# Dummy products, smaller first loads, second-scale sums between blocks, and a last row tile on VectorE in a hybrid encoder layer

## The chip, the cores and the metric

The kernel runs on one core of a Trainium2 chip. The metric is device time in microseconds (us), the median of repeated runs. A core has five engines that run their own instruction streams and wait for each other through semaphores: TensorE (PE in the profile; its weight loads are listed apart as PEld), VectorE (DVE), ScalarE (ACT), GpSimd (POOL) and SyncE (SP), which here only issues transfers. Sixteen DMA engines carry the transfers.

## The reference

One layer of an encoder, batch 1, 1024 positions, width 2048, float32 throughout:

```
h   = rmsnorm(x, pre_g) * (1 + scale(c)) + shift(c)      # shift, scale, gate = silu(c) @ w_ada + b_ada
q, k, v, gate_a, u, gate_p = split(h @ w_in)              # w_in: 2048 x 4608
y_a = windowed_attention(q, k, v; relative bias, sink) * silu(gate_a)
y_p = multi_scale_pool(u) * silu(gate_p)
g   = sigmoid(h @ w_merge + b_merge)                      # 2048 x 4096
m   = g_a * (y_a @ w_br_attn) + g_p * (y_p @ w_br_pool)
out = x + gate(c) * rmsnorm(m @ w_out, post_g)
```

## The kernel before

Every large product keeps float32 accuracy by splitting both operands into a high part and a low rest (`hi`, `lo`) and adding three products, high by high, low by high and high by low. ScalarE makes the high part (a copy to `F32R`), VectorE the low one (source minus high). Most products are also done by a seven-product scheme on 2 x 2 blocks (`strassen`); TensorE runs these nearly without a gap from about 80 us to the end.

The change concerns the two ends of the program.

**The ramp.** Before `h` is known, the kernel has to load x (8 MB) and to get the modulation. It avoids waiting for either. `fetch_scales(j)` loads the columns of `w_ada` for the scale of 256 channels (pair j: contraction tiles k = 2j and 2j + 1) as eight tiles of 256 KB. `row_sums` multiplies them with silu(c) on TensorE: step q takes four of the sixteen contraction tiles (two transfers), with four of them side by side in column groups of the array; the last step copies the sums to `acc` on ScalarE, and the step after it (`sum_columns`) transposes them (PM), reduces them on VectorE, and `scale_columns` writes the factors `modc`. Meanwhile x is loaded and transposed on TensorE (`turn_part`, line 502, into `XT`), and `raw_operands` multiplies the transposed tile with its `modc` column while it splits it: the high part on ScalarE (line 695), the low on VectorE (line 696). So the products of the first 256 output columns (key and value columns of `w_in`, the `wide` tiles) can run on scaled, not yet normalized x (`plain_block`, line 833; `PB` in the profile). The factors of the rows follow when all of x has been squared (`square_of`, `norm_row`, `factors`), and are spread over columns by two products with `ones` (`spread_factors`, RB). From then on the modulation for further channels, the transposes of the rest and the first `strassen` products (`ramp_gen`) follow.

A `plain_block(i, blk, j)` makes one 128 x 512 block from six products: number n = 0 and 1 are high by high for the two contraction tiles kh = 0 and 1 of pair j, 2 and 3 use the low weights, 4 and 5 the low x. Block "11" and "21" are for the first 512 positions, "12" and "22" for the last 512. Operand names: B11 and B21 are the two contraction tiles for the first positions, B12 and B22 those for the last.

Instructions wrapped in `keep` stay in the order in which the program writes them, on each engine; this holds for nearly all of the ramp. All loads of the ramp go through SP's queue, in program order. In the head this order is: the eight tiles of scale 0; columns 0 to 255 of x for the first four row tiles (four transfers of 128 KB); the first 256 columns of `wide`; columns 0 to 511 of the last four row tiles (256 KB each); columns 256 to 511 of the first four; the other 256 columns of `wide`; the eight tiles of scale 1; the next `wide` tile; then the remaining columns of x.

**The end.** `out_pair` makes the last output rows. For the last two row tiles (t = 0, 1), once the last product is there, `square` sums its squares on ScalarE, `scale_of` gives the row factor, and each of the four 512-column blocks is finished by `r * scale + x` and stored. `finish_block` does this in one VectorE instruction and stores through SP's queue; for one block of the very last tile `finish_apart` does it with ScalarE (multiply), GpSimd (add) and ScalarE's queue (store).

The lines that the steps below speak of: 539 products of `row_sums`, 543 `acc`, 523 transposes of the sums, 695/696 `raw_operands`, 562 loads of scales, 437 loads of x columns (`fetch_halves`), 847 `put_by`, 187 loads of weights for `strassen`, 96 the high part in `split`, 293 the copy into Z in `strassen`, 1737/1738 `finish_block`, 1742 to 1744 `finish_apart`.

## Time and profile before

| | |
|---|---|
| runs | 2085.36, 2086.59, 2087.91 us; median 2086.59 |
| profiled execution | 2086.87 us; its span 2085.1 us |
| busy: TensorE, VectorE, ScalarE, GpSimd | 2066.5, 1566.2, 1112.1, 39.4 us |
| chain of work that ended last | TensorE 93%, DMA 3%, VectorE 2%, ScalarE 1% |
| granted TensorE clock | 0.999 |
| DMA | 476.61 MB, mean 229 GB/s |

How to read the lines below. A line of the timeline is: start in us from the span's start, length in us, engine, line of the kernel, operation, `out<-in` by the program's names, shapes, count (xN merges N instructions that follow each other), and in brackets how long the engine sat idle before it and what ended that. A q behind an engine (SPq) marks an instruction of its queue, such as the issue of a transfer. A matmul in float32 appears as two instructions. A line of the table by stretch is: the stretch, its length, the busy time of PE, PEld, DVE, ACT and POOL with the number of instructions, the granted clock, the DMA share and GB/s. A line of waits is: who waited, for whom, us in total, times, longest. A line of transfers is: `out<-in`, queue, count, size, median us from issue to landing.

### The profile page before, as it was taken

The numbers are of one execution on the slowest core, as the hardware profiler recorded it, in microseconds if no ns is written. First come the engines' busy times: TensorE is split into PE (matmuls) and PEld (weight loads), VectorE is DVE, ScalarE is ACT, GpSimd is POOL, SyncE is SP. The second block draws the span as 40 slices with busy tenths as digits, with TensorE's granted clock in tenths as the row PEclk, the third lists the DMA queues.
The fourth block names the chain that finished last, engine by engine and source line by source line (L and its number), as shares of the span: only waits on it lengthen the run. The fifth ranks groups of instructions, "written<-read, shape, count | busy, mean of one in ns | idle before, by whom it ended". The sixth has DMA issues, their size and how long they took to land.

```text
span 2085.1 us, 29058 instructions
## 1 busy us (share of the span) xinstructions
PE 2066.5 (99%) x9527; PEld 1701.9 (82%) x9527; DVE 1566.2 (75%) x2822; ACT 1112.1 (53%) x2121; POOL 39.4 (2%) x133
## 2 busy tenths in 40 slices
PE   8999999999999999999999999999999999999998
PEld 6678888888888888888888888888888888888886
DVE  5889688776565876777777788858858977889667
ACT  5764444444664634656665443334645645768554
POOL 0100000000000000000000000010000000000000
PEclk9999999999999999999999999999999999999999
DMA  9978877887575477655554576675654556786996
GB/s 342 357 269 268 267 248 249 291 287 227 189 236 168 161 260 257 205 166 176 183 169 149 179 235 224 201 243 191 227 168 162 189 186 205 239 295 211 299 335 231
DMA packets 303137, 476.61 MB, mean 229 GB/s; under 512 B 24026, under 2 KB 140402, under 8 KB 302984
## 3 DMA queue, kind: packets, MB, share of 16 engines
q1 hardware_dynamic: 297472, 459.63, 67.2%
q0 software_dynamic: 4304, 12.75, 1.6%
q10 hardware_dynamic: 1208, 2.37, 0.3%
q8 instruction: 75, 1.23, 0.2%
q14 instruction: 78, 0.64, 0.1%
HBM read 346.70 MB, written 130.05 MB: 229 GB/s over the span
## 4 chain that ended last, share of the span: by engine, by line
PE 93%; DMA 3%; DVE 2%; ACT 1%; issue 0%; SPq 0%; DVEq 0%; ACTq 0%
PE Z L237 31%; PE V L237 21%; PE X L237 20%; PE Z L1704 2%; PE Z L1706 2%; PE Z L1705 2%; PE X L1704 1%; PE V L1706 1%; PE X L1706 1%; PE V L1704 1%; PE V L1705 1%; PE X L1705 1%; DMA raw<-in_w_merge_dram 1%; PE PB L833 1%; PE PT L1414 1%; DMA raw<-in_w_in_dram 1%
## 5 line engine op out<-in xcount | busy, mean ns | idle before, releaser
L96 ACT ACTIVATE whi<-raw 128x512 fp32r<-128x512 f32 (+1 forms) x528 | 314.6, 600 | 490.4 <-PE Z L237 245.5
L97 DVE TENSOR_TENSOR wlo<-raw,whi 128x512 fp32r<-128x512 f32 (+1 forms) x528 | 339.5, 648 | 135.9 <-PE Z L237 102.5
L97 DVE TENSOR_TENSOR wlo<-wr,whi 128x512 fp32r<-128x512 f32 x224 | 150.5, 688 | 52.1 <-ACT whi L96 49.2
L96 ACT ACTIVATE whi<-wr 128x512 fp32r<-128x512 f32 x224 | 138.4, 629 | 87.6 <-DVE wlo L97 29.6
L103 DVE TENSOR_TENSOR raw<-raw,raw 128x512 f32<-128x512 f32 x76 | 52.4, 690 | 89.7 <-DMA raw<-in_w_merge_dram 59.6
L96 ACT ACTIVATE whi<-ws 128x512 fp32r<-128x512 f32 (+1 forms) x88 | 53.0, 602 | 71.3 <-PE X L237 62.3
L237 PE MATMUL V<-T3h,whi 128*128 128x512 f32 x328 | 89.6, 392 | 1.0 <-DVE u L103 0.9
L237 PE MATMUL Z<-B22h,whi 128*128 128x512 f32 x328 | 89.6, 392 | 0.0
L237 PE MATMUL Z<-T1h,whi 128*128 128x512 f32 x328 | 89.6, 390 | 0.0
L237 PE MATMUL X<-B21h,whi 128*128 128x512 f32 x328 | 89.5, 391 | 0.0
L237 PE MATMUL Z<-T2h,wlo 128*128 128x512 f32 x328 | 88.9, 390 | 0.6 <-DVE wlo L97 0.6
L237 PE MATMUL X<-B11h,whi 128*128 128x512 f32 x328 | 89.4, 390 | 0.0
L237 PE MATMUL Z<-T2h,whi 128*128 128x512 f32 x328 | 89.0, 390 | 0.4 <-ACT Z L293 0.3
L237 PE MATMUL V<-T4h,whi 128*128 128x512 f32 x328 | 89.3, 391 | 0.0
L237 PE MATMUL X<-B11l,whi 128*128 128x512 f32 x328 | 89.2, 390 | 0.0
L237 PE MATMUL Z<-B22l,whi 128*128 128x512 f32 x328 | 88.9, 390 | 0.0
L237 PE MATMUL Z<-T1l,whi 128*128 128x512 f32 x328 | 88.9, 389 | 0.0
L237 PE MATMUL V<-T3l,whi 128*128 128x512 f32 x328 | 88.9, 390 | 0.0
L237 PE MATMUL X<-B21l,whi 128*128 128x512 f32 x328 | 88.9, 390 | 0.0
L237 PE MATMUL V<-T4l,whi 128*128 128x512 f32 x328 | 88.8, 390 | 0.0
L237 PE MATMUL V<-T4h,wlo 128*128 128x512 f32 x328 | 88.8, 390 | 0.0
L237 PE MATMUL X<-B11h,wlo 128*128 128x512 f32 x328 | 88.8, 390 | 0.0
(423 smaller groups left out, 4910.9 us busy)
## 6 DMA issues: line engine op xcount, KB each, us to landing
part<-part_d SPq DMA_DIRECT2D x136, 256.0 KB, 4.9
ada<-in_w_ada_dram SPq DMA_DIRECT2D x128, 256.0 KB, 5.9
raw<-in_w_merge_dram SPq DMA_DIRECT2D x64, 512.0 KB, 5.3
wr<-ws_dS SPq DMA_DIRECT2D x60, 512.0 KB, 5.5
raw<-in_w_in_dram SPq DMA_DIRECT2D x56, 512.0 KB, 4.3
wr<-in_w_out_dram SPq DMA_DIRECT2D x48, 512.0 KB, 5.5
proj_d<-part SPq DMA_DIRECT2D x68, 256.0 KB, 2.3
sw<-in_w_out_dram SPq DMA_DIRECT2D x64, 256.0 KB, 5.3
```

The lines of the kernel that those rows point to most:

```text
L96: ins = (nc.scalar.activation(hi, src, AF.Copy), nc.vector.tensor_tensor(lo, src, f32(hi), ALU.subtract))
L97: nc.vector.tensor_tensor(lo, src, f32(hi), ALU.subtract))
L103: return (eng or nc.vector).tensor_tensor(o, a, b, ALU.add)
L237: nc.tensor.matmul(ps, w_[:, i], op[mov][j][m_], start=fresh and i == 0 and n == 0, stop=i == nj - 1 and n == 2, skip_group_check=True)
L833: keep(nc.tensor.matmul(opened[i, blk], w[:, kh, nt * P:(nt + 1) * P], mov[kh][m], start=j == n == 0, stop=j == 1 and n == 5, skip_group_c ...
L1414: nc.tensor.transpose(pt[:, i * P:(i + 1) * P], p[:, i * P:(i + 1) * P], ident)
L1704: nc.tensor.matmul(pb, hi, w[0], start=first, stop=False, skip_group_check=True)
L1705: nc.tensor.matmul(pb, lo, w[0], start=False, stop=False, skip_group_check=True)
L1706: nc.tensor.matmul(pb, hi, w[1], start=False, stop=last, skip_group_check=True)
```

## The change

- Before the first product, six dummy products of `ones` by `ones` (128 x 128, float32) are put on TensorE, then three more after the transpose of c, and one more after each of the first two steps of the first scale's sums. `ones` is set by VectorE instead of GpSimd for that, ahead of `scz`.
- The first columns of x and of `wide` are loaded by contraction tile: columns 0 to 127 of four row tiles and the weights of the first contraction tile, then columns 128 to 255 and the second. The last four row tiles come in halves of 256 columns. Weights and x operands are split by contraction tile too (`first_weights`, `raw_operands` with `khs`).
- The first scale's sums (`g[4]`) are put ahead of the first transposes of x. The product numbers of the first two blocks run in the order 0, 2, 4, 1, 3 and then 5, where it was 0, 2, 1, 3 and then 4, 5.
- The second scale's sums are put between blocks: two steps, the six products of block "11", two steps, four products of block "21", the transposes of the sums, the last two products. The two `square_of` steps that stood ahead of them come after. The high weights of the second 256 columns (`wide_weights(1, 0)`) are made before the transposes instead of after them.
- `finish_apart` goes; `finish_block` does all four blocks of the last row tile, in the order 0, 2, 3, 1.

```diff
@@ -385,9 +385,9 @@
     fetch_rows(rows, b_ada[0, 0:2 * D], pre_g[0])
     nsink_t = const.tile([P, NH], F32, name="nsink_t")
     scz = xa2.tile([P, KT, 32], F32, name="scz")
+    ones = xa2.tile([P, P], F32, name="ones")
+    nc.vector.memset(ones, 1.0)
     nc.vector.memset(scz, 0.0)
-    ones = xa2.tile([P, P], F32, name="ones")
-    nc.gpsimd.memset(ones, 1.0)
     b1 = xa2.tile([P, 4], F32, name="b1")
     shz = xa2.tile([P, 4, 32], F32, name="shz")
     nc.gpsimd.memset(shz, 0.0)
@@ -430,11 +430,11 @@
             xts[si, q] = slot("xt", F32)
             keep(load(xts[si, q], x[si * P:(si + 1) * P, q * 512:(q + 1) * 512]))
 
-    def fetch_halves(h):
-        for si in range(4):
-            if h == 0:
+    def fetch_cols(sis, c0, c1):
+        for si in sis:
+            if (si, 0) not in xts:
                 xts[si, 0] = slot("xt", F32)
-            keep(load(xts[si, 0][:, h * 256:(h + 1) * 256], x[si * P:(si + 1) * P, h * 256:(h + 1) * 256]))
+            keep(load(xts[si, 0][:, c0:c1], x[si * P:(si + 1) * P, c0:c1]))
 
     def claim_turned(ks):
         for k in ks:
@@ -686,9 +686,10 @@
 
     right = {}
 
-    def raw_operands(j, s, turned=False):
-
-        for kh, name in enumerate(("B11", "B21") if s == 0 else ("B12", "B22")):
+    def raw_operands(j, s, turned=False, khs=(0, 1)):
+
+        for kh in khs:
+            name = (("B11", "B21") if s == 0 else ("B12", "B22"))[kh]
             k = 2 * j + kh
             src, a = tbanks[s, k] if turned else xT[k, s], modc[:, 1, kh, j:j + 1]
             hi, lo = right[j] if name == "B12" else op[name][j]
@@ -764,25 +765,34 @@
 
     raws, wide = [], {}
 
-    def fetch_wide(half, j, n1=0, n2=512):
-
-        if n1 == 0:
+    def fetch_wide(half, j, n1=0, n2=512, k0=0, k1=2):
+
+        if n1 == k0 == 0:
             wide[half, j] = wp.tile([P, 2, 512], F32, tag="raw", name=uid("wide"), bufs=4)
         n0 = COL_K + half * 512
-        keep(load(wide[half, j][:, :, n1:n2],
-                  w_in[2 * j * P:(2 * j + 2) * P, n0 + n1:n0 + n2].rearrange("(k p) n -> p k n", p=P)))
-
+        keep(load(wide[half, j][:, k0:k1, n1:n2],
+                  w_in[(2 * j + k0) * P:(2 * j + k1) * P, n0 + n1:n0 + n2].rearrange("(k p) n -> p k n", p=P)))
+
+    def warm(n):
+
+        b = bank("at", "WARM")
+        for _ in range(n):
+            keep(nc.tensor.matmul(b[:, 0:P], ones, ones, start=True, stop=True))
+
+    warm(6)
     pc = bank(SEEDED[1], "pc")
     keep(nc.tensor.transpose(pc[:, 0:16], crow, ident[0:16, 0:16]))
     keep(nc.scalar.activation(scz[:, :, 0], pc[:, 0:16], AF.Silu))
     keep(nc.scalar.activation(sc, pc[:, 0:16], AF.Silu))
+    warm(3)
     scales = [fetch_scales(0)]
-    fetch_halves(0)
-    fetch_wide(0, 0, 0, 256)
-    for si in range(4, 8):
-        fetch_row(si, (0,))
-    fetch_halves(1)
+    for k in range(2):
+        fetch_cols(range(4), k * P, (k + 1) * P)
+        fetch_wide(0, 0, 0, 256, k, k + 1)
+    fetch_cols(range(4, 8), 0, 256)
     fetch_wide(0, 0, 256, 512)
+    fetch_cols(range(4, 8), 256, 512)
+    fetch_cols(range(4), 256, 512)
     claim_turned(range(4))
     for j in range(2):
         claim(j, ("B11", "B21", "B22"))
@@ -806,14 +816,18 @@
 
     weights0 = {}
 
-    def wide_weights(i, j, by_vector=False):
+    def first_weights(kh):
+        if kh == 0:
+            weights0[0, 0] = [wp.tile([P, 2, 256], F32R, tag=t, name=uid(t), bufs=4) for t in ("whi", "wlo")]
+        hi, lo = (t[:, kh] for t in weights0[0, 0])
+        keep(nc.vector.tensor_copy(hi, wide[0, 0][:, kh, 0:256]))
+        low_weights(lo, wide[0, 0][:, kh, 0:256], hi)
+
+    def wide_weights(i, j):
         hi, lo = (wp.tile([P, 2, 256], F32R, tag=t, name=uid(t), bufs=4) for t in ("whi", "wlo"))
         src = wide[i // 2, j][:, :, i % 2 * 256:i % 2 * 256 + 256]
         weights0[i, j] = hi, lo
-        if by_vector:
-            keep(nc.vector.tensor_copy(hi, src))
-        else:
-            keep(nc.scalar.activation(hi, src, AF.Copy))
+        keep(nc.scalar.activation(hi, src, AF.Copy))
         return partial(low_weights, lo, src, hi)
 
     def low_weights(lo, src, hi):
@@ -847,12 +861,6 @@
         keep(nc.scalar.activation(t, opened.pop((i, blk)), AF.Copy))
         nc.gpsimd.dma_start(block(ramp_d[i], 0)(blk), t)
 
-    def warm(n):
-
-        b = bank("at", "WARM")
-        for _ in range(n):
-            keep(nc.tensor.matmul(b[:, 0:P], ident, ident, start=True, stop=True))
-
     BLOCKS = ("11", "21", "12", "22")
 
     given = []
@@ -881,27 +889,29 @@
         plain_block(i, blk, 1)
 
     g = row_sums(scz, scales[0], partial(scale_columns, 0), 2)
-    g[0]()
-    g[1]()
+    for q in range(2):
+        g[q]()
+        warm(1)
     g[2]()
     small_vectors()
     g[3]()
+    g[4]()
     turn_part(0, (0,), SEEDED[:1])
-    g[4]()
     turn_part(0, (1,), SEEDED[1:])
-    wide_weights(0, 0, True)()
-    raw_operands(0, 0, True)
+    for kh in range(2):
+        first_weights(kh)
+        raw_operands(0, 0, True, (kh,))
     for k in range(2):
         take_turned(0, k, k == 1)
     PAIR = (("11", "sc"), ("21", "sc"))
     for blk, tag in PAIR:
         plain_block(0, blk, 0, tag, (0,))
-    for n in (2, 1, 3):
+    for n in (2, 4, 1, 3):
         for blk, _ in PAIR:
             plain_block(0, blk, 0, None, (n,))
     turn_part(1, (0, 1), ("at", "at"))
     for blk, _ in PAIR:
-        plain_block(0, blk, 0, None, range(4, 6))
+        plain_block(0, blk, 0, None, (5,))
     raw_operands(0, 1, True)
     for k in range(2):
         take_turned(1, k, k == 1)
@@ -910,27 +920,30 @@
         plain_block(0, blk, 0, tag, range(2))
     for blk, _ in PAIR:
         plain_block(0, blk, 0, None, range(2, 6))
+    low = wide_weights(1, 0)
     turn_part(1, (2, 3), ("at", "at"))
     turn_part(0, (2, 3), SEEDED)
     for n in (1, 0):
         for k in (2, 3):
             take_turned(n, k, k == 3)
-    wide_weights(1, 0)()
+    low()
+    g = row_sums(scz, scales[1], partial(scale_columns, 1), 2)
+    g[0]()
+    g[1]()
+    plain_block(1, "11", 0, SEEDED[0])
+    g[2]()
+    g[3]()
+    plain_block(1, "21", 0, SEEDED[1], range(4))
+    g[4]()
+    plain_block(1, "21", 0, None, range(4, 6))
     for si in range(2):
         square_of(si, 0, si % 2 == 1)
-    g = row_sums(scz, scales[1], partial(scale_columns, 1), 2)
-    for step in g[:4]:
-        step()
-    plain_block(1, "11", 0, SEEDED[0], range(2))
-    g[4]()
     wide_weights(0, 1)()
     raw_operands(1, 0)
     raw_operands(1, 1)
     for si in range(2, 8):
         square_of(si, 0, si % 2 == 1)
     keep(nc.scalar.activation(ep.tile([P, 1], F32, name="root"), eps_t, AF.Sqrt))
-    plain_block(1, "11", 0, None, range(2, 6))
-    plain_block(1, "21", 0, SEEDED[1])
     wide_weights(1, 1)()
     norm_row(0)
     plain_block(0, "11", 1)
@@ -1737,12 +1750,6 @@
         keep(nc.vector.scalar_tensor_tensor(r, r, scale, xrow.pop((T, n)), op0=ALU.mult, op1=ALU.add))
         store(rows_of(T, n), r)
 
-    def finish_apart(T, n, scale):
-        r = held.pop((T, n))
-        keep(nc.scalar.activation(r, r, AF.Copy, scale=scale))
-        nc.gpsimd.tensor_tensor(r, r, xrow.pop((T, n)), ALU.add)
-        nc.scalar.dma_start(rows_of(T, n), r)
-
     def fetch_x_block(T, n, tile_of):
         xrow[T, n] = tile_of("xr")
         return load(xrow[T, n], x[T * P:(T + 1) * P, n * 512:(n + 1) * 512])
@@ -1866,9 +1873,7 @@
                 out_mm(bz[t], op, "B22", j, t, w, False, j == len(last_weights) - 1)
             result("12", t, bz[t], c12[t])
             scale = scale_of(6 + t, rest[t])
-            if t == 1:
-                finish_apart(6 + t, 3, scale)
-            for n in (0, 2, 1) if t == 1 else (0, 2, 3, 1):
+            for n in (0, 2, 3, 1):
                 finish_block(6 + t, n, scale)
 
     nextm, nextt2 = [], {}
```

## The prediction

> **What bounds the kernel now.** I read the page's busy table and chain first, then a table by stretch, then the waits of TensorE, then the timelines of the first 80 us and the last 15.
>
> ```profile
> span 2085.1 us, 29058 instructions
> PE 2066.5 (99%) x9527; PEld 1701.9 (82%) x9527; DVE 1566.2 (75%) x2822; ACT 1112.1 (53%) x2121; POOL 39.4 (2%) x133
> PE 93%; DMA 3%; DVE 2%; ACT 1%; issue 0%; SPq 0%; DVEq 0%; ACTq 0%
> ...
> 9.50:14.50 5.00, 4.02 (x28) 1.91 (x24) 1.73 (x7) 1.21 (x3) 0.00 (x0) 1.00 0.94 301
> 16.00:20.00 4.00, 3.92 (x22) 2.94 (x21) 2.55 (x5) 1.96 (x4) 0.00 (x0) 1.00 1.08 360
> 40.00:65.00 25.00, 25.00 (x128) 17.77 (x127) 20.96 (x45) 19.21 (x42) 4.15 (x27) 1.00 1.05 393
> 65.00:98.00 33.00, 32.56 (x174) 23.93 (x173) 26.26 (x60) 24.40 (x50) 4.25 (x8) 1.00 1.08 361
> 98.00:110.00 12.00, 12.00 (x72) 7.69 (x71) 9.63 (x22) 8.59 (x17) 0.00 (x0) 1.00 0.43 150
> ```
>
> TensorE is busy for 99% of the span and is 93% of the chain. The change touches only the first 30 us and the last 10. In the stretches (length, then busy time of each engine, granted clock, DMA share, GB/s) from 16 to 98 us the DMA engines are full (1.05 to 1.08); after that they have room (0.43). So there are two runners in the first 98 us, TensorE and the DMA, and a head start of one alone is worth nothing if the other decides a wait later. The profiled execution took 2086.87 us, 1.77 more than its span, and 0.28 more than the median of the runs, 2086.59.
>
> ```profile
> PE Z L237 <- ACT Z L293: 0.3, 1, 0.3
> ...
> 64.42 0.60 ACT L847 ACTIVATE c<-PB 128x512 f32<-128x512 f32 x1 [1.20 <-PE PB L833]
> 65.54 0.42 ACT L96 ACTIVATE whi<-raw 128x256 fp32r<-128x256 f32 x1 [0.51 <-DMA raw<-in_w_in_dram]
> ...
> 77.26 0.74 PE L237 MATMUL Z<-T2h,whi 128*128 128x512 f32 x2 [0.29 <-ACT Z L293]
> ```
>
> One of the few waits that the profile counts for TensorE in the first 90 us is 0.3 us at 77.26, for ScalarE's copy into Z. The chain leads from that copy back to 65.54, where ScalarE sat 0.51 us idle until a `raw` transfer landed; before it ScalarE had copied `c` at 64.42, for which it had waited 1.20 us on TensorE. So at 65.54 the DMA decides, and TensorE's own work is only 0.51 us behind it. What the head of the kernel is worth is settled there.
>
> **The change, part by part.**
>
> *Dummy products (six, three, one and one, 128 columns each).*
>
> ```profile
> 3.77 1.85 PE L539 MATMUL GEMV<-ada,scz 128*32 128x256 f32 x8 [0.29 <-ACT sc L778]
> 6.95 3.73 PE L539 MATMUL GEMV<-ada,scz 128*32 128x256 f32 x16 [1.32 <-DMA ada<-in_w_ada_dram]
> 10.85 0.84 PE L539 MATMUL GEMV<-ada,scz 128*32 128x256 f32 x8
> ...
> ada<-in_w_ada_dram SPq DMA_DIRECT2D x1, 256.0 KB, 6.7
> ...
> 50.51 1.88 PE L490 MATMUL RB<-diag,ones 128*128 128x512 f32 x4
> ```
>
> Two tiles of the first scale take 1.85 us at the start and 0.84 us at 10.85: products run at half rate until about 10.8 us, although the granted clock reads 1.00 throughout. No row shows a dummy; the nearest are the float32 sums at 50.51, two products of 512 columns in 1.88 us, so 128 columns take 0.24 us, or 0.47 at half rate. Nine before the first tile are 2.1 to 4.2 us from about 1.1 us on (when `ones` is set), so they end by 5.3 at the latest; two tiles at 0.93 more is 7.2, against 6.95, where the third tile's products start after 1.32 us of waiting for the DMA. The eighth tile's transfer is issued at about 4.3 us and lands 6.7 us later, at 11.0; the last group runs there already at full rate. So the dummies can win nothing at its end: the cover is the landing of the scale tiles. I take 0; bounds 0 and +0.2 (should the last dummy delay the eighth tile's products). If that landing came sooner, they would be worth at most the 0.5 us by which one tile is slower at half rate (0.93 against 0.42).
>
> *Sums before the transposes; x and weights by contraction tile.*
>
> ```profile
> 11.73 0.38 ACT L543 ACTIVATE acc<-GEMV 128x256 f32<-128x256 f32 x1 [7.95 <-PE GEMV L539]
> 12.66 0.38 PE L523 MATMUL PM<-ident,acc 128*128 128x128 f32 x2
> 14.41 0.73 PE L833 MATMUL PB<-B11h,whi 128*128 128x512 f32 x2 [0.93 <-ACT B11h L695]
> 16.35 1.03 PE L502 MATMUL XT<-ident,xt 128*128 128x128 f32 x8
> 17.37 0.69 ACT L695 ACTIVATE B12h<-XT,modc 128x512 fp32r<-128x512 f32 x1 [1.28 <-PE XT L502]
> ```
>
> The sums (PM) could start when `acc` is done, at 12.1, but stand behind four transposes that wait for x; now they go first: 12.66 becomes 12.16, and modc, B11h and the first product come 0.5 us earlier, 13.9. Then the gain goes: two low products now precede the eight transposes at 16.35, and B12h waits for those. Before, 14.41 to 16.35 held eight products (1.94 us); now ten (2.4): 13.9 + 2.4 = 16.3. B12h (0.69 us of ScalarE) stays at 17.3 and the next blocks, which wait for it, at 18.1. Gain at 18.1: 0.05, taken as 0. VectorE casts half a tile twice instead of one whole; its sum is the same.
>
> The price is on SP's queue. Between the first scale tiles and the second there were 14 transfers; now there are 23, of the same bytes: eight of 64 KB instead of four of 128, and more halves.
>
> ```profile
> SPq L437 <- DMA ada<-in_w_ada_dram: 1.4, 2, 0.8
> ...
> 11.88 0.90 SPq L437 DMA_DIRECT2D xt<-in_x_dram  x2
> 14.45 4.91 SPq L562 DMA_DIRECT2D ada<-in_w_ada_dram  x8
> 2079.73 0.33 SPq L1738 DMA_DIRECT2D out_dram<-c  x1
> ...
> ada<-in_w_ada_dram SPq DMA_DIRECT2D x1, 256.0 KB, 5.0
> out_dram<-c SPq DMA_DIRECT2D x1, 256.0 KB, 2.5
> ```
>
> The issues of x wait for landings of scale tiles (1.4 us, two waits); the issue times fit a limit of eight transfers under way, so smaller ones put fewer bytes under way. By the landing of the eighth tile (11.0) both kernels have issued eight more. Before, six others followed and the second scale started at 14.45. Now fifteen follow, at a pitch of 0.47 us (two in 0.90 at 11.88): 11.4 + 15 x 0.47 = 18.45. A tile of the second scale landed 5.0 us after its issue because some 2 MB stood ahead of it; with less ahead it can land after 2.5, as the last store does: 20.95 against 19.45. So everything behind on this full queue is 1.5 us late, up to the `raw` transfer at 65.54. Bounds: 0 (a pitch of 0.37, from the 0.33 of the last store's issue: 11.4 + 5.55 + 2.5 = 19.45) and +2.0 (0.50). I take +1.5, since the issues at 11.88 are of the same rows. DMA path at 65.54: +1.5.
>
> By the Trainium skill, page "DMA: Bandwidth & Descriptors", section "Measured (HBM→SBUF, 128 partitions, SWDGE, issued from GpSimd)", a 64 KB transfer reaches 138 GB/s; as an estimate from that figure, eight of them one at a time are 3.8 us where the full rate needs 1.5, and the DMA path would be +3.8 in place of +1.5. No row here shows a 64 KB transfer.
>
> *Second scale's sums between blocks.*
>
> ```profile
> 23.16 2.11 PE L539 MATMUL GEMV<-ada,scz 128*32 128x256 f32 x32
> 25.78 0.42 PE L523 MATMUL PM<-ident,acc 128*128 128x128 f32 x2
> 26.83 0.72 ACT L695 ACTIVATE B11h<-xT,modc 128x512 fp32r<-128x512 f32 x1 [0.23 <-DVE modc L550]
> 28.34 0.39 PE L833 MATMUL PB<-B11h,whi 128*128 128x512 f32 x1
> ...
> 36.13 0.58 ACT L837 ACTIVATE held<-PB 128x512 f32<-128x512 f32 x1
> 36.76 0.50 PE L833 MATMUL PB<-B12h,whi 128*128 128x512 f32 x1
> ```
>
> Before: 32 products to 25.2, two of block "11", the sums at 25.78, then ten products of cover, and B11h of the second pair at 26.83; TensorE uses it at 28.34. Now six products stand between the halves and four behind them, so the sums start after ten block products, not two: 23.16 + 2.0 + 10 x 0.23 = 27.4, and B11h at 28.45, with only two products of cover. That is +1.6 for B11h, which TensorE now waits for. From there ScalarE works nearly without a gap to the copy at 36.13 that TensorE waits for at 36.76, so +1.6 passes on. It saves about 0.3 us of waits for the last scale tiles, inside that number, and it covers the tiles' later landing: the eighth is needed 1.4 us later than before. At 64.42 the ScalarE copy comes +1.6 late: it ends at 66.6, 1.1 past 65.54. TensorE path there: +1.1; bounds 0 (should idle time between 36.8 and 64 take it up) and +1.6.
>
> At 65.54 the later one counts: max(+1.5, +1.1) = +1.5. From there to 77.26 and on nothing in the change makes it up.
>
> *Last row tile by VectorE alone.*
>
> ```profile
> 2073.24 0.75 DVE L1737 SCALAR_TENSOR_TENSOR c<-c,st,xr 128x512 f32<-128x512 f32 x1
> ...
> 2076.62 1.41 DVE L1737 SCALAR_TENSOR_TENSOR mo<-mo,st,xr 128x512 f32<-128x512 f32 x2
> 2077.43 1.73 POOL L1743 TENSOR_TENSOR p<-p,xr 128x512 f32<-128x512 f32 x1 [56.82 <-ACT p L1742]
> 2077.95 1.75 DVE L1737 SCALAR_TENSOR_TENSOR c<-c,st,xr 128x512 f32<-128x512 f32 x1
> ```
>
> The last VectorE step took 1.75 us beside GpSimd's addition, where the same step took 0.75 at 2073.24. Now four steps follow from 2076.62: 1.41 for two and 0.67 for each of two more, 2.75 in all, so 2079.37 instead of 2079.70: -0.33. Bounds: 0 (should the last step stay at 1.75 by its own doing) and -1.0 (the whole difference of 1.75 to 0.75). The last store no longer meets one of ScalarE's queue: another -0.1, an estimate. I take -0.4.
>
> **Sum.** +1.5 - 0.4 = +1.1: 2086.87 becomes 2088.0 in the profile, and the median 2087.7.
>
> **The rivals.**
> 1. *The head is hidden.* Issues take 0.37 and idle time takes up ScalarE's lateness (VectorE and ScalarE are busy 0.84 and 0.77 of 40 to 65 us); then only the tail is left: -0.4, 2086.2. Against it: 0.5 us at 65.54 is all the slack that the rows show.
> 2. *The head gains.* The DMA wins back what it lost from 9.5 to 14.5 (301 GB/s against 360 after), the `raw` transfer lands sooner, and the 0.51 us at 65.54 goes: -0.9, 2085.7. More it can't be, since ScalarE's copy of `c` ends there at 65.0.
> 3. *Slower by over 0.2%.* The small transfers run at latency, eight at a time: if each takes the 5.0 us of the row above, eight in 5.0 are 0.62 each; fifteen are 9.4 us, the second scale is issued at 20.8 and, if it again lands 5.0 later, is 6.3 late: 2086.6 + 6.3 - 0.4 = 2092.5. It decides from 4.6 us of lateness on. For it: the queue did wait for landings. Against it: those 5.0 us are mostly bytes ahead, since the last store takes 2.5. With the Trainium skill's figure above for 64 KB the time would lie between, 2090.0.
>
> **How the numbers follow.** Forecast 0.58, head hidden 0.2, head gains 0.1, latency 0.07, elsewhere 0.05. The likeliest gives 2087.7 (its own range 2086.7 to 2088.7). Head gains at 2085.7 less the 0.4 by which a median of such runs wanders gives the low end, 2085.3; 2.0 of DMA lateness with 0.5 of other waits and the same 0.4 gives 2089.6. A measurement tells 0.2%, 4.2 us; so the first three cases are the same by it, the latency is slower, and of elsewhere 0.02 is faster and 0.01 slower: faster 0.02, same 0.90, slower 0.08.
>
> **What would show it.** The first product near 13.9 and B12h still at 17.3; 23 issues between the scales, the second scale's first issue near 18.4 and its landing near 21; B11h of the second pair near 28.4 with a TensorE wait of about 0.8 us before it; the `raw` copy of 65.54 near 67; Z of 77.26 near 78.8; the last step of 0.75 us. It is wrong if the first issue of the second scale stays below 16.5, if Z is at 77.3 or earlier, or if TensorE's time between 98 us and the last product changes by more than 0.5 us.

## The result, and the profile after

The median of the changed kernel is 2090.88 us (2088.29 to 2093.76, ten runs) against 2085.97 for the kernel before on the same chip; ratio 1.0021, 95% interval 1.0012 to 1.0029, so 2.5 to 6.0 us slower. The forecast was 2087.7. Run again later, unchanged, it gave 2089.23 against 2087.53, ratio 1.0013 (1.0003 to 1.0024). The profiled execution took 2091.53 us. From its page:

```profile
span 2089.7 us, 29111 instructions
PE 2072.7 (99%) x9549; PEld 1705.7 (82%) x9549; DVE 1567.1 (75%) x2826; ACT 1111.4 (53%) x2120; POOL 37.5 (2%) x131
```

Its table by stretch (length, busy time of PE, PEld, DVE, ACT, POOL with counts, granted clock, DMA share, GB/s):

```profile
9.50:14.50 5.00, 4.14 (x25) 2.51 (x25) 2.92 (x10) 2.24 (x4) 0.00 (x0) 1.00 0.70 197
16.00:20.00 4.00, 3.62 (x17) 2.33 (x16) 2.00 (x3) 2.38 (x4) 0.00 (x0) 1.00 0.90 275
40.00:65.00 25.00, 25.00 (x123) 17.60 (x122) 20.07 (x47) 20.47 (x47) 4.07 (x27) 1.00 1.05 393
65.00:98.00 33.00, 32.75 (x180) 24.25 (x177) 26.16 (x59) 24.32 (x49) 4.35 (x11) 1.00 1.09 363
98.00:110.00 12.00, 12.00 (x70) 7.68 (x69) 10.79 (x23) 9.48 (x20) 0.00 (x0) 1.00 0.64 226
```

TensorE is again busy for 99%. The loss stands in the first two stretches: the DMA engines, at 301 and 360 GB/s before, move 197 and 275, with a share of 0.70 and 0.90. From 40 us on they are as full as before, so what was lost is not won back; more is left over for 98 to 110 (0.64 in place of 0.43).

The timeline of SP's queue (start, time spent issuing, number), and further down of what waits for those transfers:

```profile
11.49 1.85 SPq L437 DMA_DIRECT2D xt<-in_x_dram  x4
13.38 0.43 SPq L773 DMA_DIRECT2D wide<-in_w_in_dram  x1
13.86 3.79 SPq L437 DMA_DIRECT2D xt<-in_x_dram  x8
17.69 4.91 SPq L562 DMA_DIRECT2D ada<-in_w_ada_dram  x8
...
13.11 0.73 PE L847 MATMUL PB<-B11h,whi 128*128 128x512 f32 x2 [0.20 <-DVE wlo L106]
16.82 0.69 ACT L696 ACTIVATE B12h<-XT,modc 128x512 fp32r<-128x512 f32 x1 [2.26 <-PE XT L502]
27.42 1.31 PE L539 MATMUL GEMV<-ada,scz 128*32 128x256 f32 x8 [0.37 <-DMA ada<-in_w_ada_dram]
30.70 0.72 ACT L696 ACTIVATE B11h<-xT,modc 128x512 fp32r<-128x512 f32 x1 [0.41 <-DVE modc L550]
31.47 0.49 PE L847 MATMUL PB<-B11h,whi 128*128 128x512 f32 x1 [0.94 <-ACT B11h L696]
68.28 0.60 ACT L861 ACTIVATE c<-PB 128x512 f32<-128x512 f32 x1 [1.20 <-PE PB L847]
68.86 0.42 ACT L96 ACTIVATE whi<-raw 128x256 fp32r<-128x256 f32 x1
80.67 0.73 PE L237 MATMUL Z<-T2h,whi 128*128 128x512 f32 x2 [0.25 <-ACT Z L293]
```

The transfers of the first 30 us (number, size, median us from issue to landing):

```profile
xt<-in_x_dram SPq DMA_DIRECT2D x12, 128.0 KB, 3.4
xt<-in_x_dram SPq DMA_DIRECT2D x8, 64.0 KB, 2.8
```

Once the first scale has landed (10.15), SP waits for no landing before 17.69 (the view of its waits from 10.5 to 17.7 us is empty) and issues these loads at one pitch, whatever their size: (13.38 - 11.49) / 4 = 0.47 us and (17.69 - 13.86) / 8 = 0.48 for 128 KB, 0.48 for the 256 KB at 13.38, 0.475 for the last of 64 KB (10.54 to 11.01 in the trace). 128 KB at this pitch are some 275 GB/s offered, 64 KB 138, while the engines could move 350 (e3 below, 10 to 14 us). They stand idle for want of requests. Small pieces are not slow on the engines themselves: those that SP had issued while the scale tiles were still under way landed one behind the other, from 10.73 to 11.61 three of 64 KB and one of 128 KB, which is 372 GB/s (landings from the trace). The second scale, first issued at 17.69 (14.45 before), has its last tile at 28.06 (24.61 before, from the trace's landings). TensorE waits for its last two tiles at 27.42, then 0.94 us for B11h at 31.47, and Z of 77.26 comes at 80.67.

On the way to Z both runners of the prediction are late. ScalarE's copy of `c` starts 37.6 us behind the second B11h in all 14 profiles of this document, so TensorE's path passes on all of its lateness: 64.42 became 68.28, +3.9, where 0.5 was slack. The `raw` transfer landed at 65.51 before and at 68.84 here, +3.3. The copy of `raw`, 65.54 before, comes at 68.86, when both are there.

The dummies did bring TensorE to full rate sooner. In the kernel before, every product of the first scale up to 10.1 us took 0.63 us, and those from 10.85 on 0.38 to 0.40; here they take 0.38 to 0.40 from 7.20 on:

```profile
7.20 0.66 PE L539 MATMUL GEMV<-ada,scz 128*32 128x256 f32 x8
```

The trace's first record of a full granted clock stands at 8.6 to 11.9 us in the seven kernels without dummies and at 4.5 to 6.8 in the seven with them; ahead of it the views read 1.00 for want of a record, which is why the prediction found 1.00 beside products at half rate. What that is worth at the end is another matter, for which see below.

The span splits into three parts: up to Z, from Z to the start of TensorE's last product, and from there to the end. Before: 77.26 + 1997.42 + 10.42. After: 80.67 + 2000.76 + 8.31. The head lost 3.4, the middle 3.3, and the tail gained 2.1. In the tail:

```profile
2085.37 0.75 DVE L1750 SCALAR_TENSOR_TENSOR c<-c,st,xr 128x512 f32<-128x512 f32 x1
2086.14 0.33 SPq L1751 DMA_DIRECT2D out_dram<-c  x1
```

The stores of the last 30 us:

```profile
out_dram<-c SPq DMA_DIRECT2D x4, 256.0 KB, 2.5
```

The last VectorE step takes 0.75 us as forecast. But from the last store's issue to the end of the span are 3.6 us (2086.14 to 2089.7) where there were 5.4 (2079.73 to 2085.1), although the store lands as fast as before. In the middle, where the program is the same, these are TensorE's longest waits from 90 us to the end, of the kernel before, of the changed one, and of its second profile (e5):

```profile
PE V L237 <- DVE u L103: 0.9, 2, 0.5
PE Z L237 <- DVE wlo L97: 0.6, 1, 0.6
```

```profile
PE V L237 <- DVE u L103: 2.0, 2, 1.6
PE Z L237 <- ACT whi L96: 1.4, 1, 1.4
PE Z L237 <- DVE wlo L97: 0.8, 1, 0.8
```

```profile
PE Z L237 <- DVE wlo L97: 0.6, 1, 0.6
PE V L237 <- DVE u L103: 0.5, 1, 0.5
```

The first profile after has 4.2 us of such waits, where the one before has 1.5 and the second one after 1.1. Whether they belong to the change had to be tested.

### The profile page after: what moved, and what is told of

It reads as the page before. It is cut to its first block, busy times and chain, and to the rows that moved or that the text cites. A ratio compares the mean times of both kernels' runs of the same rounds, so it can differ in the third digit from the quotient of the medians.

```text
span 2089.7 us, 29111 instructions
## 1 busy us (share of the span) xinstructions
PE 2072.7 (99%) x9549; PEld 1705.7 (82%) x9549; DVE 1567.1 (75%) x2826; ACT 1111.4 (53%) x2120; POOL 37.5 (2%) x131
## 4 chain that ended last, share of the span: by engine, by line
PE 93%; DMA 3%; DVE 2%; SPq 1%; ACT 1%; issue 1%; DVEq 0%; ACTq 0%
PE Z L237 31%; PE V L237 21%; PE X L237 20%; PE Z L1717 2%; PE Z L1719 2%; PE Z L1718 2%; PE V L1719 1%; PE V L1718 1%; PE X L1718 1%; PE X L1719 1%; PE X L1717 1%; PE V L1717 1%; PE PB L847 1%; DMA ada<-in_w_ada_dram 1%; DMA raw<-in_w_merge_dram 1%; PE PT L1427 1%
## 5 line engine op out<-in xcount | busy, mean ns | idle before, releaser
L103 DVE TENSOR_TENSOR u<-V,u 128x512 f32<-128x512 f32 x94 | 64.6, 687 | 33.7 <-PE V L237 29.8
```

Source lines behind the costliest of these rows:

```text
L103: return (eng or nc.vector).tensor_tensor(o, a, b, ALU.add)
```

## The experiments

Theory A: the 23 small loads starve the DMA engines and are the head's loss. Theory B: the second scale's sums between the blocks cost 1.1 to 1.6 by themselves. Theory C: the end of the program waited for GpSimd. D1: the middle's loss is chance; D2: it belongs to the change. One profile was taken of each kernel; landings are from its trace. The experiments e3, e4 and e6 start from the kernel before, e9, e10 and e12 from e3, the others from the changed kernel. Ratios and differences of times are to the kernel before, run beside each. The pieces of code are shortened: `...` marks what is left out, and short lines are joined by semicolons.

| kernel | transfers between the scales | first scale's last tile | second scale: first issue | its last tile | second B11h | Z | Z to last product | to the end |
|---|---|---|---|---|---|---|---|---|
| before | 14 | 11.01 | 14.45 | 24.61 | 26.83 | 77.26 | 1997.42 | 10.42 |
| e3, tail alone | 14 | 10.34 | 13.88 | 23.44 | 26.09 | 76.06 | 1998.05 | 8.53 |
| e9, tiny GpSimd | 14 | 10.85 | 15.36 | 24.72 | 26.94 | 78.32 | 1998.05 | 8.68 |
| e8, loads and sums back | 14 | 10.10 | 13.60 | 24.03 | 26.25 | 77.37 | 1997.81 | 8.45 |
| e1, loads back | 14 | 10.04 | 13.57 | 24.16 | 27.84 | 77.83 | 1995.94 | 8.55 |
| e12, nine loads | 9 | 10.37 | 11.76 | 23.18 | 28.94 | 78.92 | 1999.53 | 8.15 |
| e6, small first | 19 | 10.27 | 16.02 | 26.53 | 28.98 | 78.96 | 1997.83 | 10.41 |
| e4, loads alone | 23 | 9.99 | 17.55 | 27.60 | 29.82 | 79.80 | 1998.52 | 10.41 |
| e2, sums back | 23 | 10.14 | 17.68 | 27.78 | 30.00 | 80.42 | 1997.47 | 8.30 |
| after | 23 | 10.15 | 17.69 | 28.06 | 30.70 | 80.67 | 2000.76 | 8.31 |
| e5, after again | 23 | 10.38 | 19.57 | 29.05 | 31.69 | 83.32 | 1996.75 | 8.31 |
| e11, GpSimd's queue | 15 + 8 | 14.33 | 18.04 | 28.54 | 33.83 | 83.81 | 1996.51 | 8.47 |
| e10, by partitions | 23 | 11.60 | 21.11 | 32.23 | 34.45 | 84.44 | 2000.02 | 8.28 |
| e7, two queues | 15 + 8 | 9.93 | 15.84 | 26.07 | 35.97 | 85.95 | 1998.19 | 8.47 |

**e4_loads_only: the loads alone.**

```diff
-    fetch_halves(0); fetch_wide(0, 0, 0, 256)
-    for si in range(4, 8): fetch_row(si, (0,))
-    fetch_halves(1)
+    for k in range(2):
+        fetch_cols(range(4), k * P, (k + 1) * P); fetch_wide(0, 0, 0, 256, k, k + 1)
+    fetch_cols(range(4, 8), 0, 256)
     fetch_wide(0, 0, 256, 512)
+    fetch_cols(range(4, 8), 256, 512); fetch_cols(range(4), 256, 512)
```

> The kernel before with nothing changed but the 23 loads in place of 14 between the two scales. Theory A: the second scale's last tile lands near 28.1 (24.6 before), Z near 80.7, the time 2089.4, or 2092 if the waits near 260 and 1640 us follow from the lateness. The prediction's term (+1.5): Z near 78.8, 2087.5. Theory B (most of the head's lateness is the sums between the blocks): Z at 77.3 to 78.8.

2091.18 us against 2087.07, ratio 1.0017 (1.0007 to 1.0027): alone they cost 4.1 us, where the whole change, with the gain of its tail, cost 4.9 and 1.7. Its SP queue, second B11h and Z, then the same of the tail alone, which has the old head:

```profile
17.55 4.07 SPq L562 DMA_DIRECT2D ada<-in_w_ada_dram  x8
29.82 0.72 ACT L695 ACTIVATE B11h<-xT,modc 128x512 fp32r<-128x512 f32 x1 [0.21 <-DVE modc L550]
79.80 0.73 PE L237 MATMUL Z<-T2h,whi 128*128 128x512 f32 x2 [0.25 <-ACT Z L293]
```

```profile
13.88 4.29 SPq L562 DMA_DIRECT2D ada<-in_w_ada_dram  x8
26.09 0.72 ACT L695 ACTIVATE B11h<-xT,modc 128x512 fp32r<-128x512 f32 x1 [0.60 <-DVE modc L550]
76.06 0.73 PE L237 MATMUL Z<-T2h,whi 128*128 128x512 f32 x2 [0.24 <-ACT Z L293]
```

All three are 3.7 us apart. A holds; the forecast's +1.5 falls.

**e1_loads_back and e2_sums_back: one part of the head undone.**

```diff
 e1:
-    for k in range(2):
-        fetch_cols(range(4), k * P, (k + 1) * P); fetch_wide(0, 0, 0, 256, k, k + 1)
...
+    fetch_cols(range(4), 0, 256); fetch_wide(0, 0, 0, 256)
+    fetch_cols(range(4, 8), 0, 512); fetch_cols(range(4), 256, 512)
+    fetch_wide(0, 0, 256, 512)
 e2:
-    g[0](); g[1]()
-    plain_block(1, "11", 0, SEEDED[0])
-    g[2](); g[3]()
...
+    for step in g[:4]: step()
+    plain_block(1, "11", 0, SEEDED[0], range(2))
+    g[4]()
...
```

> The changed kernel with the 14 loads of the kernel before between the two scales. Theory A (the 23 small loads starve the DMA engines; they are the whole lateness of the head): the Z product that stood at 77.26 before and at 80.67 after returns to 77.3 or a little earlier, since the first product still comes near 13.1; the last raw copy of the head stands near 65.5. Theory B (the second scale's sums between the blocks cost 1.1 to 1.6 by themselves): Z at 78.4 to 78.9. By A with the tail's -2.1 the time is near 2084; by B near 2085.3. If the extra waits near 260 and 1640 us (+3 in the changed kernel) follow from the head's lateness, they are gone here; if they come from somewhere else or by chance, TensorE again loses 1 to 3 us there.

> The changed kernel with the second scale's sums in one piece, two products of block 11 ahead of the transposed sums and ten behind, as before. Theory A: Z stays at 80.7 and the time near 2090.9, for the second scale's last tile still lands at 28. Theory B: Z near 79.2 and the time near 2089.4. A third outcome: Z later than 80.7, since TensorE then stands waiting for the late tiles with no block between: up to +1.4, 2092.3.

e1: 2088.85 against 2087.07, ratio 1.0007 (0.9998 to 1.0017); e2: 2089.69, 1.0010 (1.0001 to 1.0018). Both theories had e1 near 2084 or 2085, and so missed its time. With the old loads the sums between the blocks do cost what B says: B11h stands 3.7 us behind the last tile's landing (24.16 to 27.84) where it stands 2.2 behind with the sums in one piece (e8, 24.03 to 26.25), +1.5.

```profile
27.84 0.72 ACT L696 ACTIVATE B11h<-xT,modc 128x512 fp32r<-128x512 f32 x1 [0.38 <-DVE modc L550]
```

```profile
26.25 0.72 ACT L696 ACTIVATE B11h<-xT,modc 128x512 fp32r<-128x512 f32 x1 [0.22 <-DVE modc L550]
```

With the new loads, whose tiles come late, they cost little: 2.6 behind (after and e5) against 2.2 (e2, e4), +0.4. So in the changed kernel B is a small part: e2, with the sums back, has Z at 80.42, near A's 80.7 and far from B's 79.2.

With the old loads B is not settled at the end of the head. The copy of `c` is 1.6 later in e1 than in e8 (65.43 and 63.84), but in e8 the `raw` transfer landed only at 65.71, so there the DMA decided, and Z is 0.5 apart (77.83 and 77.37; A had 77.3, B 78.4 to 78.9). The times are further apart: e1 lies 1.8 above the kernel before, e8 1.3 below it. The profile of e1 is of the fastest of its twelve runs (2084.10), and the intervals of the two overlap, so how much of these 3.1 us is B stays open.

**e6_small_first: 19 transfers.**

```diff
-    fetch_halves(0); fetch_wide(0, 0, 0, 256)
+    for k in range(2):
+        fetch_cols(range(4), k * P, (k + 1) * P); fetch_wide(0, 0, 0, 256, k, k + 1)
```

> The kernel before with only the first part of the small loads: x columns 0 to 255 of rows 0 to 3 as eight of 64 KB and the first weights as two of 64 KB (19 transfers between the scales in place of 14), the 256 KB transfers of rows 4 to 7 whole as before. If the queue pays by the transfer (0.47 us of issue each, while fewer bytes are under way), the lateness is 5/9 of the 3.7 that the 23 loads cost alone: second scale's first issue near 16, Z near 78.1, 2 us slower than before. If only the 128 KB halves of the later rows matter: Z at 76.1 to 77.3. If only the 64 KB transfers matter: Z near 79.8.

2090.08, ratio 1.0012 (1.0002 to 1.0022). (The two transfers of the first weights are of 128 KB, not 64 as the expectation has it.)

```profile
16.02 4.97 SPq L562 DMA_DIRECT2D ada<-in_w_ada_dram  x8
28.98 0.71 ACT L695 ACTIVATE B11h<-xT,modc 128x512 fp32r<-128x512 f32 x1
```

The second scale is issued at 16.02, between 13.9 and 17.6, as a price by the transfer asks. (Z, at 78.96, is less clear: 78.1 was expected, and 79.8 if only the 64 KB transfers mattered.) Counted from the landing of the first scale's last tile, the time to that issue is (transfers - 7) x 0.474: 3.3 for 14 (measured 3.4 to 3.5 in four profiles, 4.5 in e9), 5.7 for 19 (5.75), 7.6 for 23 (7.5 to 7.6 in three, 9.2 in e5), 3.8 for 15 (3.7 in e11). The last tile lands 9.4 to 10.6 us after the first issue in all of these, whatever stood ahead. Three kernels do not fit, each for a reason that its trace shows: e12 (0.9 reckoned, 1.4 measured), where SP waits for a landing before each of these issues; e7 (3.8 and 5.9), where it waits 1.8 us for one; and e10 (7.6 and 9.5), where an issue takes longer. The last tile of e6, 26.53, lies 0.6 of the way from 24.2 (mean of the five kernels with 14) to 28.1 (mean of the four with 23 other than e10); 5/9 was expected.

**e12_nine_loads: fewer than before.**

```diff
+    for si in range(4): fetch_row(si, (0,))
+    fetch_wide(0, 0)
     for si in range(4, 8): fetch_row(si, (0,))
```

> The kernel with only the tail changed, and nine transfers in place of 14 between the scales: rows 0 to 3 whole (256 KB each), the first weights whole (512 KB), rows 4 to 7 whole. If the price of a transfer is paid only while pieces are so small that 0.47 us of issue moves less than the engines could (some 166 KB at 350 GB/s), there is little left to win: second scale's last tile at 23.0 to 24, Z at 76 to 77, or up to 1 later, since the first product now waits for 1.5 MB behind the scale tiles (near 15.5). If every transfer cost its share even here (3.7 us for nine of them), Z would be 2 us earlier, near 74 to 75.

2087.60, ratio 0.9998 (0.9989 to 1.0008).

```profile
11.76 5.79 SPq L562 DMA_DIRECT2D ada<-in_w_ada_dram  x8
15.05 0.96 PE L832 MATMUL PB<-B11h,whi 128*128 128x512 f32 x2 [0.93 <-ACT B11h L695]
```

By stretch:

```profile
10.00:14.00 4.00, 2.49 (x16) 1.31 (x14) 0.25 (x2) 0.38 (x1) 0.00 (x0) 1.00 1.05 400
14.00:18.00 4.00, 3.07 (x10) 2.14 (x9) 3.41 (x7) 1.86 (x3) 0.00 (x0) 0.67 1.08 370
```

The tail alone (e3), from 10 to 14 us:

```profile
10.00:14.00 4.00, 3.04 (x20) 1.74 (x21) 1.86 (x7) 1.34 (x3) 0.00 (x0) 1.00 1.04 350
```

The first issue is 2.1 us earlier than with the tail alone, yet the last tile lands only 0.3 earlier: at 400 GB/s the engines are full, and the price by the transfer is gone, as expected. Z is later by 2.9, more than expected, since the transposes wait for x, the first product starts at 15.05 (13.78 with the tail alone), and the clock then falls. TensorE reaches the sums of the second scale late: B11h stands 5.8 us behind the last tile's landing, where it is 2.2 in the kernels in which the tiles decide (e8, e2, e4).

**e10_by_partitions: 23 transfers without narrower rows.**

```diff
-                load(xts[si, q], x[si * P:(si + 1) * P, ...])
+            for a, b in ((0, 64), (64, P)):
+                load(xts[si, q][a:b], x[si * P + a:si * P + b, ...])
```

> The kernel with only the tail changed, and its first nine loads after the scale tiles cut in two by partitions (64 rows each), so that again 23 transfers stand in place of 14, but no row of a transfer is narrower than before. If the price is by the transfer (issue pitch, and the limit of eight under way): second scale's first issue near 17.6, its last tile near 27 to 28, Z 2.5 to 3.7 later than with the tail alone (79 to 80), time 2 to 4 us above the tail alone. If it is the narrow rows (512 and 1024 bytes in place of 1024 and 2048) that the DMA engines move more slowly: last tile near 24, Z at 76 to 77.5. If half as many rows are also issued in half the time: first issue near 14, Z as with the tail alone.

2090.06, ratio 1.0016 (1.0006 to 1.0025); the profile is of the slowest of its ten runs.

```profile
13.46 5.08 SPq L432 DMA_DIRECT2D xt<-in_x_dram  x8
21.11 4.20 SPq L565 DMA_DIRECT2D ada<-in_w_ada_dram  x8
```

By stretch:

```profile
10.00:14.00 4.00, 2.42 (x15) 0.88 (x13) 0.38 (x2) 0.38 (x1) 0.00 (x0) 0.94 0.37 102
```

Narrow rows are not needed for the loss. From 10 to 14 us the DMA share is 0.37. Its head is even later than that of the changed kernel, in part because its first scale landed 1.4 us later. The rest is in the main the pitch: the eight issues at 13.46 took 5.08 us, 0.64 each in place of 0.474, though each has half the rows (64 of 128) of the transfer from which it was cut. So the price is by the transfer here too, but it is not the same for every form, and issuing half the rows took more time and not half of it.

**e7_two_queues and e11_gpsimd_queue: the last eight small loads on another queue.**

```diff
-    fetch_cols(range(4, 8), 256, 512)
-    fetch_cols(range(4), 256, 512)
+    fetch_cols(range(4, 8), 256, 512, nc.scalar.dma_start)   # e11: nc.gpsimd.dma_start
+    fetch_cols(range(4), 256, 512, nc.scalar.dma_start)
```

> The changed kernel with its last eight loads between the scales (the right halves of x's first column block, 128 KB each) issued on ScalarE's queue, so that SP's queue reaches the second scale eight transfers sooner, with the same bytes and the same pieces in all. If SP's issue and its limit of transfers under way are what starves the DMA engines: second scale's first issue near 13.9, its last tile near 24, Z near 77.8 to 78.5 (what is left is the sums between the blocks), the stretch from 10 to 22 us back above 300 GB/s. If the small pieces are slow by themselves on the DMA engines: the last tile again near 28, Z near 80.7. A danger: the eight on the other queue share the engines with the first scale's tiles, which then land up to 1.4 us later, and the first product comes that much later.

> The changed kernel with its last eight loads between the scales issued on GpSimd's queue, which has nothing else to do there and whose transfers do not count among SP's eight. Same bytes, same pieces. If SP's queue is what starves the engines: second scale's first issue near 13.9, its last tile near 24 to 25, DMA share from 10 to 22 us back near 1.0; the first scale's tiles may land up to 2.8 us later, since 1 MB more is under way beside them, and the first product with them (near 16). Z then at 77.5 to 79. If small pieces are slow by themselves: last tile at 27 to 28 and Z near 80.7 or later.

2094.32, ratio 1.0035 (1.0025 to 1.0046), and 2092.26, 1.0026 (1.0015 to 1.0037): both worse, and neither settles what it was made for, whether small pieces are slow by themselves. (The landings given with the result do: they are not.) ScalarE's queue in e7, and the DMA rows of e11:

```profile
9.18 7.57 ACTq L437 DMA_DIRECT2D xt<-in_x_dram  x8
16.80 0.38 ACT L543 ACTIVATE acc<-GEMV 128x256 f32<-128x256 f32 x1 [12.27 <-DMA xt<-in_x_dram]
```

```profile
18.04 4.06 SPq L562 DMA_DIRECT2D ada<-in_w_ada_dram  x8
```

By stretch:

```profile
14.00:18.00 4.00, 3.52 (x18) 2.21 (x16) 1.25 (x5) 0.83 (x2) 0.00 (x0) 0.50 0.59 169
```

In e7 ScalarE's own issues waited for landings from 9.18 to 16.75, and its copy `acc`, next in its order, came at 16.80 in place of 10.87: the first product moved from 13.1 to 19.6. In e11 the eight loads did go out early, beside the first scale, whose last tile then landed at 14.33 (the larger loss that was named as a danger). SP still had eight issues left and needed 3.7 us for them, during which the engines moved 169 GB/s at a share of 0.59. So the starved stretch moved and did not go, which fits A, but the last tile's 28.54 is also what the other theory gave. Z tells nothing in either: B11h stands 9.9 us (e7) and 5.3 us (e11) behind the last tile's landing, since TensorE itself came late, at a granted clock of 0.50 from 14 to 18 us.

**e3_tail_only and e9_tiny_gpsimd: the tail.**

```diff
 e3: -    if t == 1: finish_apart(6 + t, 3, scale)
     +    for n in (0, 2, 3, 1): finish_block(6 + t, n, scale)
 e9: e3, and
     +    if t == 1: nc.gpsimd.tensor_tensor(tiny, scale, eps_t, ALU.add)   # 128 x 1
```

> The kernel before with nothing changed but the last row tile: four VectorE steps, no GpSimd addition, no store on ScalarE's queue. Theory C (the closing of the program waited for GpSimd's 6.9 us drain, which this takes away): from the last VectorE step's end to the end of the span 3.6 us in place of 5.4, 2.1 less in all, median near 2083.9. The prediction's term: -0.4, near 2085.6. Z stays at 77.3, and the waits near 260 and 1640 us are those of the kernel before if they depend on the head; if they are chance, they differ by 1 to 3 us.

> The kernel with only the tail changed (all four blocks of the last row tile on VectorE), and beside them one addition of 128 x 1 on GpSimd, into a tile that nothing reads. Theory C1 (GpSimd's closing drain takes some 5 us after its last late operation, whatever the size): the end of the span comes again about 10 us after TensorE's last product begins (10.42 in the kernel before, 8.5 with the tail alone), a little less because the tiny addition starts sooner. Theory C2 (the drain writes back what the 128 x 512 addition left, or waits for ScalarE's store): 8.5 stays.

e3: 2085.84 against 2087.07, ratio 0.9987 (0.9979 to 0.9996), the lowest ratio here; by the medians -1.2, where theory C had -2.1 and the prediction -0.4. From the last product to the end the profile has 8.53 in place of 10.42: -1.9. e9 (one run, 2086.91) adds one small addition on GpSimd:

```profile
2078.36 0.75 POOL L1871 TENSOR_TENSOR tiny<-st,eps_t 128x1 f32<-128x1 f32 x1 [56.05 <-DVE st L1732]
```

It ends at 2079.11, and the span, 2085.05 long, ends 5.94 later. In the kernel before it was 2079.16 and 2085.10: 5.94 again; in e4 and e6, with the large addition, 5.94 as well. The trace names the instruction: GpSimd's DRAIN ends 5.15 us behind its last addition in all four (2079.16 to 2084.31 before, 2079.11 to 2084.26 in e9), for 128 x 512 and for 128 x 1, and the end of the program follows 0.8 us later. In e3 the drain is over at 2027.98, and the end follows SP's last wait. So what counts is when GpSimd's last operation ends. In e9 it ended early enough to cost only 0.15 against e3: its drain was over 0.1 us after SP's last wait (2084.15). The mechanism of C1 holds; its 10 us did not come, because the tiny addition ended sooner than was reckoned.

**e5_after_again and e8_old_loads_sums: the middle, and what is left.**

e5 has no edit; e8 has the edits of e1 and e2 together:

```diff
+    fetch_cols(range(4), 0, 256); fetch_wide(0, 0, 0, 256)
...
+    for step in g[:4]: step()
...
```

> The changed kernel once more, unchanged, for a second profile. Theory D1 (the extra 3 us between 98 us and the last product are waits that wander from run to run): TensorE's stretches from 105 to 283 us (177.1 to 179.0 in the profiles so far) and from 1620 to 1646 us (25.9 to 28.1) come out anywhere in those ranges, Z again near 80.7. Theory D2 (they belong to the change): 179 and 28 again. Time by D1 near before + 2 (head +4.0 against the mean of two profiles with the old head, tail -2.0), by D2 near before + 5.

> The changed kernel with both losing parts undone: loads of the kernel before, second scale's sums in one piece; what stays of the change is the dummies, the first sums ahead of the transposes, and the tail by VectorE. Z between 75.5 and 76.5 (76.06 and 77.26 in the two profiles with the old head), for the first product at 13.0 comes 0.8 sooner but the loads set the end of the head; tail -2.0; time 2 to 3 us below before. If the head's gain counts in full, Z near 75.3; if the dummies and the sums' place are worth nothing, it is the time of the kernel with the tail alone.

e5: 2089.23, ratio 1.0013 (1.0003 to 1.0024). The middle takes 1996.75, the shortest but two of 14 profiles, where the first profile after has the longest, 2000.76. The 14 run from 1995.94 to 2000.76 with no order by the head: 1998.05 with Z at 76.06, 1996.51 with Z at 83.81. That fits D1 and not D2; what makes the middle wander is not shown. Z was not "again near 80.7": SP spent 5.43 us on the eight issues that took 3.79 in the first profile, because the last of them took 2.07 (why is open), and the second scale began at 19.57.

```profile
14.10 5.43 SPq L437 DMA_DIRECT2D xt<-in_x_dram  x8
19.57 4.03 SPq L562 DMA_DIRECT2D ada<-in_w_ada_dram  x8
```

e8: 2086.24 against 2087.53, ratio 0.9992 (0.9983 to 1.0001). It has the first product at 13.06, 0.7 before that of the tail alone, and the second B11h at 26.25, 0.2 behind it: B11h waits for the second scale, whose last tile landed 0.6 later than in e3, so dummies and the order of the sums leave nothing there. Z, at 77.37, missed the expected 75.5 to 76.5, since the `raw` transfer landed only at 65.71 and ScalarE waited 1.30 us for it. The time is 1.3 below the kernel before, where 2 to 3 was expected. The version with the lowest ratio is the kernel before with the new tail (e3), though its interval and that of e8 overlap.

## Why the prediction was wrong

- **Dummies 0: right, as far as the runs show.** They brought the full rate 3.6 us sooner (7.20 in place of 10.85), but the first scale's end is set by the landing of its eighth tile: ScalarE's copy `acc` starts 0.72 us behind it with dummies (after, e1, e2, e5, e8) and without (before, e4, e6, e12, e10). In two kernels without them, e3 and e9, it starts 0.94 and 1.16 behind; up to 0.4 us could have been won there. The landing itself wanders by more, 10.04 to 11.01 in the five profiles with 14 loads.
- **Sums first, gain gone by B12h: right.** B11h and the first product came 1.3 earlier, 0.86 of it by an earlier eighth tile; at B12h it was 0.55, less than that tile alone; in e8 nothing was left at 26 us.
- **23 transfers, +1.5: the step that failed.** Its first half held: 18.45 less the 0.86 by which the eighth tile came sooner is 17.59, and 17.69 was measured. The second half, "with less ahead it can land after 2.5, as the last store does", did not: the first tile took 4.1 us from issue to landing (17.69 to 21.81), in e2 4.7 and in e4 4.0, and the last tile landed 9.4 to 10.6 after the first issue in old and new heads. The first tile, by which I reckoned, came 2.4 later than before (19.40 to 21.81); TensorE waits for the last, and for that one no part of the later issue came back, where I subtracted 2.5. The term is 9 x 0.474 = +4.3, which lies beyond the bound of +2.0 that I gave. Less the 0.86 of an eighth tile that happened to land sooner it is 3.4, and the last tile came 3.45 later, the `raw` transfer of 65.54 3.3 and Z 3.4. Against the tail alone e4 measured +3.7 at Z.
- The figure of the Trainium skill, page "DMA: Bandwidth & Descriptors", section "Measured (HBM→SBUF, 128 partitions, SWDGE, issued from GpSimd)", 138 GB/s for 64 KB, would have given +3.8 by the estimate above. (The same row of the page gives 0.95 us for such a transfer, which would be twice that.) The trace is near it in the size of the loss, but by coincidence: 64 KB at a pitch of 0.475 us are 138 GB/s too, and since transfers of 128 and 256 KB keep that pitch, and 64 KB pieces landed at 372 GB/s where enough of them were under way, here it is the issue on SP's queue that sets it (the page measured GpSimd's).
- **Sums between blocks, +1.6 as a path of its own: right in size, wrong in place.** e1 shows +1.5 at B11h, and it was passed on whole as far as the copy of `c` (+1.6). But I reckoned the DMA's lateness to come in at 65.54 only, and took the later of two paths there, while TensorE's path itself starts from the late tiles: the sums add 0.4 to them, and TensorE carries all of it to 65.54.
- **Tail -0.4: mis-sized.** VectorE's part was right: its last step took 0.75 us and ended 4.68 us behind the start of the last product, where it was 5.02, so -0.34 (-0.33 reckoned). The -0.1 for a store that meets no other shows in no run: the last store took 2.5 us to land before, 2.4 to 2.6 since. The term left out what GpSimd's addition does to the end of the program, 1.6 to 1.8 us more. Measured -1.9 to -2.1. In the rows of before it could be seen: 5.4 us from the last store's issue to the end, with 2.5 to its landing.
- **The test by TensorE's time behind 98 us was none**: that time (from Z on in the table) wanders by 4.8 us with the same instructions.
- **The rivals.** Head hidden and head gains fell with Z at 80.67. The third had the right sign and the wrong mechanism: the small transfers took 2.8 and 3.4 us, not 5.0, and were issued at the pitch, not at a latency; the price is 0.474 us for each transfer, and the DMA's lateness stayed under the 4.6 us from which that rival decided.
- **The range.** Its upper end does not come out of its own terms: 2.0 of DMA lateness, 0.5 of waits and 0.4 of wander on 2086.6 give 2089.1 with the tail's -0.4 and 2089.5 without it, not 2089.6. The measured 2090.88 lies beyond either.

With the measured terms the sum is +4.3 + 0.4 - 2.0 = +2.7. The two comparisons gave +4.9 (2.5 to 6.0) and +1.7 (0.6 to 5.0). Both intervals hold it. That the first lies 2 higher is not explained; the head (80.67 and 83.32 in the two profiles) and the middle wander by as much.

## What to carry to other kernels

Where a queue is full, count its transfers and not only its bytes: each costs the pitch of its issue (0.474 us here, 0.64 in e10), so pieces smaller than pitch x rate leave the DMA engines idle (an estimate from these runs: 0.474 us x 350 GB/s = 166 KB), and everything issued behind them is late by the whole of it. A piece that arrives sooner helps only if the end of that stage waits for it. At the end of a program, give no last operation to an engine whose closing is slow (GpSimd here, 5.15 us), and compare two profiles of the same code before a difference in an unchanged part is believed.

## What the runs showed of the hardware that was not expected

- GpSimd's last operation ends 5.94 us before the end of the span in the four kernels that have one late, for 128 x 512 and for 128 x 1; 5.15 of it is the DRAIN behind it.
- Issues on ScalarE's queue waited for landings too and held ScalarE for 7.57 us (e7).
- An issue of half the rows (64 partitions in place of 128) took longer on SP's queue, 0.64 us in place of 0.474 (e10).
- The granted clock fell where TensorE was only thinly used. In e12 it was 0.67 from 14 to 18 us, although no idle gap of TensorE before it was longer than 0.93 us; busy from 10 to 14 was 2.49 of 4 us (3.04 with the tail alone, where the clock stayed at 1.00). In e10 it was 0.50 from 14 to 18, and the longest wait before was 0.9. The Trainium skill, page "TensorE: Matmul & The Clock Gate", section "Part 1: The HAM clock gate (the "warmup" mystery)", has the clock halve after an idle window of some 3.4 us. The traces differ: in e7, where TensorE stood still from 10.6 to 17.2 us, the clock was halved from 12.6 on, 2.0 us after the last product, and e12 and e10 had no idle stretch of even 1 us.
